# A decoder layer on one core: 28 chunks of u turned during the mixer, none in the gates' stage, and the softmax's maximum taken right behind the last logits

## The chip, the core and the metric

The kernel runs on one NeuronCore of a Trainium2 chip. The core has TensorE (PE in the profile; its weight loads are PEld), VectorE (DVE), ScalarE (ACT), GpSimd (POOL) and SyncE (SP). The metric is the device time of one execution in microseconds (us); lower is better.

## The reference

One layer over 256 tokens of width 1024, in float32:

```python
h = rmsnorm(x, mix_norm_g); proj = h @ w_in          # nine groups of columns
ret = retention(rotary(rq), rotary(rk), rv); y_a = (ret * silu(rg)) @ ret_w_branch
att = moba_attention(norm(mq), norm(mk), mv, rel_bias)   # softmax over 256 keys, 8 heads
y_b = att @ moba_w_branch
x = x + (sigmoid(ga) * y_a + sigmoid(gb) * y_b) @ w_out
h2 = rmsnorm(x, ffn_norm_g)
# product keys: 8 heads, 16 of 128 x 128 experts for each token
a = gelu(einsum('td,thkd->thk', h2, u_tab[experts]))
x = x + einsum('thk,thkd->td', gates * a, v_tab[experts])
```

The tables `peer_u` and `peer_v` hold 16384 rows of 1024 numbers each (64 MB).

## The kernel before, in words

**Stages.** The mixer (0 to about 250 us) computes everything up to the residual. The stage of the queries (to about 297) multiplies by `peer_w_q`. The gates' stage (297 to 638) multiplies the activations with all of `peer_u`, in 128 chunks of 128 experts, for most of the tokens, applies gelu and the gates; the last stage does the same with `peer_v` and ends with the output. For the remaining tokens the rows of their experts are gathered one by one (`fetch`, L1056, issued by POOL; the dot products are on DVE, L1067), six buffers in a ring.

**The mixer's order.** The weights come in pieces of 256 x 512 numbers (0.5 MB). At step `i` of the loop at L851 the program issues, in this order: the loads of pieces up to four ahead (SP, L208, into `raw_ring`, a ring of six buffers), `cut(i + 3)` (the high half of a piece on ACT, L153, the low half on DVE, L154), the products of piece `i` on TensorE (L236 to L238), `early_turns(i)`, and `pump()`, which advances up to three side tasks by one `yield` each. Attention is such a task. Each engine works its instructions off in the order in which they were issued.

**Attention (L356).** For each of two tiles of 128 tokens: the logits of eight heads (L367), the bias added by DVE (L371, a `yield` after each group of heads), in the next step the maximum on DVE (L375) and four exponentials on ACT (L377), then four more, then the transposes of the probabilities on TensorE (L389).

**Chunks of u must be transposed.** Most are turned on TensorE in the gates' stage: `transpose_u(c + 2)` at L1315 gives eight transposes of 128 x 128 (L734) and two copies on ACT (L735), two chunks ahead of the products at L1333. Two other ways spare TensorE this:

- *Turned in the mixer* (`early_turns`, L761): chunk `EARLY[m]` is loaded by four DMAs of POOL (L744) at step `TURNED[m] - 4`, turned by DVE in two halves at steps `TURNED[m]` and the next (L748), and written to the DRAM buffer `turned` by a DMA that ACT issues two steps after `TURNED[m]` (L771). The gates' stage loads it back into `raw_ring` and multiplies straight from there. There are three pairs of buffers in turn (`SLOT`): `eraw` and `eT`; `h2` and `hTf`; and a third that is half of `sa` and half of `ret` at first, and from chunk number `LATE` on the attention's tile `pr`.
- *Turned in the gates' stage* (`TURN`): chunks 124 and 126 are loaded by ACT's queue in quarters, beside the products of chunks 95 to 109 (L1323 to L1328), and turned by DVE (L727).

14 chunks (`HELD`) lie in W from the queries' stage on. The other chunks come through `raw_ring`, in order, by SP (L676, or L699 for those turned early); an early chunk keeps its buffer until its product, two chunks longer than the others.

**The gates' stage beside it.** A list of tasks with due times (`chain_step`) first finds the top experts and then builds the dense gates: one-hot factors on DVE (L1194, L1197) and ACT (L1201), their products on TensorE (L1252, L1253), the evacuation on ACT (L1268) and DVE (L1270), and the product with gelu on POOL (L1285). `gather` issues a little over one row fetch for each chunk.

Of the kernel before, what the change touches and what calls it, by code (L numbers as in the profile page):

```python
# [11 lines left out]
F32 = mybir.dt.float32  # L12
# [7 lines left out]
OP = mybir.AluOpType  # L20
AX = mybir.AxisListType

P = 128
# [3 lines left out]
KC = D // P  # L27
H = 8
# [22 lines left out]
HELD = [0, 1, 2, 8, 14, 21] + list(range(26, 62, 6)) + [61, 66]  # L51
HELD0 = 2
FOLD = 104
TURNED = [8, 10, 12, 14] + list(range(20, 34, 2)) + [37, 40, 42, 45, 47, 50, 52, 55, 57, 60, 62, 65, 67, 70]
NPRE = len(TURNED)
LEAD = 4
LATE = 13
SLOT = [m % 3 for m in range(11)] + [m % 3 for m in range(NPRE - 11)]
EARLY = [c for c in range(3, 121) if c not in HELD]
EARLY = [EARLY[round(m * (len(EARLY) - 1) / (NPRE - 1))] for m in range(NPRE)]  # L60
TURN = (124, 126)
TURN0 = 95
WARM = 8
GROW = 96
VX = 14
# [16 lines left out]
def layer_kernel(ctx, tc, x, mix_norm_g, w_in, ret_w_branch, moba_q_gain, moba_k_gain, moba_w_branch,  # L82
# [33 lines left out]
    def hi_tile(dt=F32R):  # L116
        return rg.tile([P, 1024], dt, name="rhi_", tag="rhi", bufs=4)

    def lo_tile(dt=F32R):
        return rg.tile([P, 1024], dt, name="rlo_", tag="rlo", bufs=4)  # L120
# [235 lines left out]
    def attention():  # L356
        ssum = wk.tile([P, NT, H], F32, name="ssum")
        for t in range(NT):
            w = (t + 1) * P
            pr = wk.tile([P, H, S], F32, name="pr")  # L360
            nh = 512 // w
            for i0 in range(0, 4, nh):
                ps = [side() for _ in range(2)]
                for j in range(nh):
                    for c in range(2):
                        b = slice(c * 64, (c + 1) * 64)
                        T.matmul(ps[c][:, j * w:(j + 1) * w], mqk[0][b, i0 + j, t * P:(t + 1) * P],  # L367
                                 mqk[1][b, i0 + j, :w], start=True, stop=True)
                for c in range(2):
                    n = slice(4 * c + i0, 4 * c + i0 + nh)  # L370
                    V.tensor_tensor(pr[:, n, :w], ps[c].rearrange("p (j k) -> p j k", j=nh),  # L371
                                    bias[:, n, S - w:], op=OP.add)
                    yield
            sm = wk.tile([P, H], F32, name="smx")
            V.tensor_reduce(sm, pr[:, :, :w], axis=AX.X, op=OP.max, negate=True)  # L375
            for h in range(H):
                A.activation(pr[:, h, :w], pr[:, h, :w], AF.Exp, bias=sm[:, h:h + 1], accum_out=ssum[:, t, h:h + 1])  # L377
                if h % 4 == 3:
                    yield
            rs = wk.tile([P, H], F32, name="rs")  # L380
            V.reciprocal(rs, ssum[:, t, :])
            yield
            turned_pr = []
            for kt in range(t + 1):
                prT = t4([P, H, P], "prT")
                for q in range(2):
                    p = side()
                    for j in range(4):
                        T.transpose(p[:, j * P:(j + 1) * P], pr[:, 4 * q + j, kt * P:(kt + 1) * P], ident)  # L389
                    A.activation(prT[:, 4 * q:4 * q + 4, :], p.rearrange("p (j i) -> p j i", j=4), AF.Copy)  # L390
                turned_pr.append(prT)
                yield
            rr, at = [pr[:, 2 * i:2 * i + 2, :].rearrange("p h k -> p (h k)") for i in range(2)]
            A.activation(rr.rearrange("p (i c d) -> p i c d", c=2, d=64),
                         rs.rearrange("p (c i) -> p i c", c=2)[:, :, :, None].to_broadcast([P, 4, 2, 64]), AF.Copy)
            yield
            if t == 0:
                yield
            po, pt = side(), side()
            for i in range(4):  # L400
                T.transpose(pt[:, i * P:(i + 1) * P], rr[:, i * P:(i + 1) * P], ident)
            for kt, prT in enumerate(turned_pr):
                for i in range(4):
                    for c in range(2):
                        h = 2 * i + c
                        T.matmul(po[c * 64:(c + 1) * 64, i * P:(i + 1) * P], mv[:, kt, h * 64:(h + 1) * 64],
                                 prT[:, 4 * c + i, :], start=(kt == 0 and i == 0), stop=(kt == t), skip_group_check=True)
            A.activation(at, pt, AF.Copy)
            yield
            V.tensor_tensor(at, at, po, op=OP.mult)  # L410
            yield
            split_to(ah[0][:, :, t * P:(t + 1) * P], al[0][:, :, t * P:(t + 1) * P],
                     at.rearrange("p (c q) -> p c q", c=4))
            yield
# [268 lines left out]
    def load_any(i):  # L683

        if sk_at <= i < sk_at + 2:
            r = raw_tile().rearrange("p (j i) -> p j i", j=H)
            nc.sync.dma_start(r, peer_sub_keys[0].rearrange("h c n d -> n (h c) d")[:, H * (i - sk_at):H * (i - sk_at + 1), :])
            sk_raw.append(r)
            return
        i -= 2 * (i >= sk_at)  # L690
        if i < len(pieces):
            load(i)
        elif i < len(pieces) + NK:
            c = i - len(pieces)
            if c in HELD or c in TURN:
                return
            if early_chunk(c):
                u_raw[c] = raw_tile()
                nc.sync.dma_start(u_raw[c], turned[EARLY.index(c)])  # L699
            else:  # L700
                u_raw[c] = load_rows(peer_u, c)
        elif i < len(pieces) + 2 * NK:
            c = i - len(pieces) - NK
            n = (c - VX) % (RAWS + 2) - RAWS if c >= VX else -1
            v_raw[c] = load_rows(peer_v, c, spare(n) if n >= 0 else None)
# [13 lines left out]
    def transpose_u(c):  # L719

        if c < NK and early_chunk(c):
            u_T[c] = u_raw.pop(c)
        elif c in TURN:
            r = u_raw.pop(c)
            u_T[c] = hi_tile(F32)
            for k in range(0, KC, 4):
                turn(u_T[c], r, slice(k, k + 4))  # L727
        elif c < NK:
            r = u_raw.pop(c)
            u_T[c] = hi_tile(F32)  # L730
            for q in range(2):
                p = side()
                for k in range(4):
                    T.transpose(p[:, k * P:(k + 1) * P], r.rearrange("p (i k) -> p k i", k=KC)[:, 4 * q + k], ident)  # L734
                A.activation(u_T[c][:, 512 * q:512 * (q + 1)], p, AF.Copy)  # L735

    def early_chunk(c):
        return c in EARLY

# [6 lines left out]
    def turn(dst, src, k):  # L746

        V.transpose(dst.rearrange("p (k b a) -> p b k a", k=KC, b=4)[:, :, k],  # L748
                    src.rearrange("p (b k i) -> p b k i", b=4, k=KC)[:, :, k])
# [561 lines left out]
    for c in range(NK):  # L1311
        load_to(len(pieces) + c + TAHEAD)
        rows_x(c)
        gates_finish()
        transpose_u(c + TAHEAD)  # L1315
        if c and c % 2 == 0:
            product_evac(c - 2, pa)
        if c == SCRATCH:
            while any(g in chain for g in topk_all):
                chain_step(1.0)  # L1320
        if c % 2 == 0:
            pa = acc(0)
        m, g = divmod(c - TURN0, 8)  # L1323
        if 0 <= m < len(TURN) and g % 2 == 0:
            if g == 0:
                assert gs["xdone"]
                u_raw[TURN[m]] = lo_tile(F32)
            load_quarters(nc.scalar, u_raw[TURN[m]], TURN[m], (g // 2,))  # L1328
        uT = u_T.pop(c)
        hT = hTd if c in TURN or early_chunk(c) else hTf  # L1330
        for k in range(KC):
            n = c % 2 * NA
            T.matmul(pa[:, n:n + NA], uT[:, k * P:(k + 1) * P], hT[:, k], start=(c % 2 == 0 and k == 0),  # L1333
                     stop=(k == KC - 1), skip_group_check=True)
        pump()
        if c < NK - 6 or gs["dot"] == NU and (not gs["weighed"] or gs["v"] - gs["sum"] < RING - 1):
            gather(gs["pace"])
        chain_step(BUDGET)

        if c == NK - 4:  # L1340
            while chain:
                chain_step(9.0)
                gates_finish()
            cw = cp.tile([P, 2, D], F32R, name="cw", tag="b8")[:, :, :4 * ND].rearrange("p s (c t) -> p s c t", c=2)
        if c >= NK - 5:
            load_to(len(pieces) + c + 3)
        if c == NK - 3:
            cut_w(0)
            cut_v(0)
        elif c == NK - 2:  # L1350
            cut_v(1)
# [143 lines left out]
```

## Time and profile before

| what | us |
|---|---|
| median of 3 runs | 934.42 (934.07 to 935.47) |
| the profiled execution | 934.2 |
| its span, first to last instruction | 932.4 |
| PE busy | 921.0 |
| DVE busy | 802.0 |
| ACT busy | 511.3 |
| POOL busy | 439.8 |

The page of the profile gives busy times, groups of instructions by line, and the chain of work that ended last. Other views of the same trace show who waited for whom, the instructions in order of time, the busy time of each engine in chosen stretches, and single lines with the landing times of their DMAs. In a row of the order of time, the brackets tell how long the engine had been idle and what ended it. Names of tiles are the program's: `raw_ring` for what SP loaded, `rhi` and `rlo` for the two halves of a piece, `rows` for gathered rows.

### The profile page before, as it was taken

Reading aid. Unit: us, or ns where it says so; the run is one execution under the profiler, and the core shown is the slowest. Engines: PE = TensorE matmul, PEld = TensorE weight load, DVE = VectorE, ACT = ScalarE, POOL = GpSimd, SP = SyncE. Lnnn points to the kernel's source line nnn. Section 1 sums busy time; section 2 is a strip of 40 time slices with the busy share of each in tenths; the row PEclk is TensorE's granted clock in tenths of the full one; section 3 lists DMA queues with packets and bytes.
Section 4 is the critical chain, followed back from the end, with each engine's and each line's share of the span. In section 5 each row is a group of like instructions: output and inputs, shape, how many; then the busy total and the mean of one; then the engine's idle time right before and its main releaser. Section 6 shows DMA issues by size and latency. Waiting matters only on the chain.

```text
span 932.4 us, 18724 instructions
## 1 busy us (share of the span) xinstructions
PE 921.0 (99%) x6960; PEld 874.1 (94%) x6960; DVE 802.0 (86%) x1537; ACT 511.3 (55%) x940; POOL 439.8 (47%) x408
## 2 busy tenths in 40 slices
PE   8999999999999999999999999899999999999998
PEld 6877888888999999999999999899999999999997
DVE  6668666888779999999999989896999989898996
ACT  5455655544644435444677776686454545454543
POOL 3617133321202447435655676674656555555530
PEclk9999999999999999999999999999999999999999
DMA  9999997999799999999999999999999999999991
GB/s 319 222 354 246 342 271 227 351 334 329 240 370 396 408 385 354 386 353 378 408 392 404 370 389 366 390 409 350 371 396 409 409 406 409 385 408 380 386 385 63
DMA packets 108121, 329.88 MB, mean 354 GB/s; under 512 B 12316, under 2 KB 17349, under 8 KB 107902
## 3 DMA queue, kind: packets, MB, share of 16 engines
q1 hardware_dynamic: 65244, 184.12, 54.6%
q0 software_dynamic: 37248, 128.00, 37.5%
q10 hardware_dynamic: 5538, 16.57, 4.6%
q8 instruction: 55, 0.90, 0.4%
q14 instruction: 36, 0.29, 0.1%
HBM read 312.30 MB, written 17.86 MB: 354 GB/s over the span
## 4 chain that ended last, share of the span: by engine, by line
PE 66%; DMA 4%; DVE 1%; POOL 1%; issue 0%; ACT 0%; DVEq 0%; POOLq 0%
PE acc L1333 20%; PE acc L1365 9%; PE side L1365 9%; PE side L734 8%; PE acc L1366 4%; PE side L1366 4%; DMA rows<-in_peer_u_dram,eg 3%; PE side L1363 2%; PE acc L1363 2%; PE acc L246 1%; PE acc L245 1%; PE acc L247 1%; DMA rows__6045<-in_peer_u_dram,eg 1%; PE side L626 1%; DMA gx<-av 1%; PE acc L1252 1%
## 5 line engine op out<-in xcount | busy, mean ns | idle before, releaser
L1056 POOL DMA_INDIRECT rows<-in_peer_u_dram,eg x86 | 104.9, 1220 | 79.4 <-DVE rows L1067 38.5
L1056 POOL DMA_INDIRECT rows<-in_peer_v_dram,eg x54 | 101.3, 1876 | 75.5 <-DVE vacc L1155 59.1
L734 PE MATMUL side<-ident,raw_ring 128*128 128x128 f32 x696 | 93.4, 277 | 0.8 <-DMA raw_ring<-in_peer_u_dram 0.8
L734 PEld LDWEIGHTS side<-ident,raw_ring 128*128 128x128 f32 x696 | 84.3, 192 | 1.1 <-PE acc L1253 0.9
L1299 ACT ACTIVATE cw<-W 128x352 fp32r<-128x352 f32 x58 | 29.0, 499 | 71.1 <-PE acc L1366 71.1
L1067 DVE SCALAR_TENSOR_TENSOR rows<-rows,h 128x1024 f32<-128x1024 f32 x44 | 54.7, 1249 | 6.7 <-DMA rows<-in_peer_u_dram,eg 6.6
L1201 ACT ACTIVATE oh_buf<-oh_more,tS 128x128 bf16<-128x128 f16 x176 | 58.5, 419 | 3.4 <-DVE oh_more L1194 3.3
L1155 DVE SCALAR_TENSOR_TENSOR vacc<-rows,av,vacc 128x1024 f32<-128x1024 f32 x42 | 53.8, 1281 | 0.1
L1333 PE MATMUL acc<-hTd,raw_ring 128*128 128x128 f32 x400 | 48.8, 275 | 0.0
L1333 PEld LDWEIGHTS acc<-hTd,raw_ring 128*128 128x128 f32 x400 | 46.7, 192 | 0.0
L1300 DVE TENSOR_TENSOR cw<-W,cw 128x352 fp32r<-128x352 f32 x58 | 30.3, 522 | 16.5 <-ACT cw L1299 16.0
L1285 POOL TENSOR_TENSOR W<-W,gl 128x256 f32<-128x256 f32 (+21 forms) x32 | 26.6, 830 | 25.1 <-ACT gl L1284 22.9
L744 POOL DMA_DIRECT2D eraw<-in_peer_u_dram x36 | 19.8, 556 | 30.8 <-DVE eT L748 30.8
L1194 DVE TENSOR_TENSOR oh_more<-iota,tI 128x1024 f16<-128x1024 f16 x44 | 33.5, 761 | 0.0
L1197 DVE TENSOR_TENSOR oh_buf<-oh_more,tM 128x1024 f16<-128x1024 f16 x44 | 33.2, 755 | 0.0
L744 POOL DMA_DIRECT2D h<-in_peer_u_dram x36 | 19.7, 554 | 23.1 <-DVE hTf L748 22.8
L1252 PE MATMUL acc<-oh_buf 128*128 128x128 bf16 x176 | 24.4, 219 | 2.7 <-DVE W L1270 2.7
L1268 ACT ACTIVATE W<-acc 128x512 f32<-128x512 f32 (+22 forms) x44 | 17.3, 393 | 17.4 <-PE acc L1253 16.4
L1253 PE MATMUL acc<-oh_buf 128*128 128x128 bf16 x176 | 24.4, 219 | 0.0
L1252 PEld LDWEIGHTS <-oh_buf 128*128 128x128 f16 x176 | 19.8, 113 | 2.9 <-DVE W L1270 2.9
L1287 ACT ACTIVATE W<-acc 128x256 f32<-128x256 f32 (+21 forms) x53 | 18.5, 350 | 4.4 <-PE acc L1333 4.3
L1270 DVE TENSOR_TENSOR W<-acc,W 128x256 f32<-128x256 f32 (+21 forms) x32 | 16.1, 502 | 4.8 <-ACT W L1268 4.8
(2608 smaller groups left out, 3400.7 us busy)
## 6 DMA issues: line engine op xcount, KB each, us to landing
raw_ring<-in_peer_v_dram SPq DMA_DIRECT2D x100, 512.0 KB, 10.1
raw_ring<-in_peer_u_dram SPq DMA_DIRECT2D x87, 512.0 KB, 9.5
raw_ring<-in_w_in_dram SPq DMA_DIRECT2D x52, 512.0 KB, 7.6
W<-in_peer_v_dram SPq DMA_DIRECT2D x28, 512.0 KB, 10.6
raw_ring<-turned SPq DMA_DIRECT2D x25, 512.0 KB, 10.7
raw_ring<-in_peer_w_q_dram SPq DMA_DIRECT2D x16, 512.0 KB, 10.8
W<-in_peer_u_dram SPq DMA_DIRECT2D x14, 512.0 KB, 11.1
eraw<-in_peer_u_dram POOLq DMA_DIRECT2D x36, 128.0 KB, 8.0
```

Source lines behind the costliest of these rows:

```text
L734: T.transpose(p[:, k * P:(k + 1) * P], r.rearrange("p (i k) -> p k i", k=KC)[:, 4 * q + k], ident)
L744: queue.dma_start(dst[32 * g:32 * g + 32].rearrange("a (b d) -> a b d", b=4), src[g])
L1056: G.indirect_dma_start(out=r, out_offset=None, in_=tab, in_offset=bass.IndirectOffsetOnAxis(ap=eg[:, j:j + 1], axis=0))
L1067: V.scalar_tensor_tensor(r, r, 1.0, h, op0=OP.mult, op1=OP.mult, accum_out=av[:, j:j + 1])
L1155: V.scalar_tensor_tensor(a, r, av[:, j:j + 1], a, op0=OP.mult, op1=OP.add)
L1194: V.tensor_tensor(hot, iota4[:, None].to_broadcast(shape), tI[:, t, :, None, k:k + 4].to_broadcast(shape), op=OP.is_equal)
L1201: A.activation(o1[:, j], hot[:, 0, :, j], AF.Copy, scale=tS[:, t, k + j:k + j + 1])
L1252: T.matmul(p[:, j * P:(j + 1) * P], hi, o1, start=True, stop=False)
L1333: T.matmul(pa[:, n:n + NA], uT[:, k * P:(k + 1) * P], hT[:, k], start=(c % 2 == 0 and k == 0), stop=(k == KC - 1), skip_group_check=True)
L1363: T.matmul(o[b][:, :ND], vh[:, n], w, start=False, stop=False, skip_group_check=True)
L1365: T.matmul(o[b][:, :2 * ND], vh[:, n], w, start=(c == 0), stop=False, skip_group_check=True)
L1366: T.matmul(o[b][:, :ND], vl[:, n], w[:, :ND], start=False, stop=(c == NK - 1), skip_group_check=True)
```

## The change

The list of steps `TURNED` gets 16, 18 and 34, so 28 chunks are turned during the mixer instead of 25. `LATE` and `SLOT` are shifted by three, so the last 14 chunks keep their steps and buffers. `EARLY` is drawn from the chunks 3 to 125 instead of 3 to 120: before it was 3, 7, 13, 18, 24, 29, 34, 40, 45, 51, 55, 62, 67, 71, 76, 80, 85, 89, 94, 98, 102, 107, 111, 116, 120; after it is 3, 7, 12, 17, 22, 28, 33, 37, 42, 47, 52, 57, 62, 67, 72, 76, 80, 84, 88, 92, 96, 100, 104, 109, 113, 117, 121, 125. `TURN` is gone: chunks 124 and 126 come through the ring and are turned on TensorE. In attention, the maximum is issued right behind the last addition of the bias, one step earlier; the exponentials stay where they were.

```diff
--- before.py
+++ after.py
@@ -51,15 +51,13 @@
 HELD = [0, 1, 2, 8, 14, 21] + list(range(26, 62, 6)) + [61, 66]
 HELD0 = 2
 FOLD = 104
-TURNED = [8, 10, 12, 14] + list(range(20, 34, 2)) + [37, 40, 42, 45, 47, 50, 52, 55, 57, 60, 62, 65, 67, 70]
+TURNED = list(range(8, 36, 2)) + [37, 40, 42, 45, 47, 50, 52, 55, 57, 60, 62, 65, 67, 70]
 NPRE = len(TURNED)
 LEAD = 4
-LATE = 13
-SLOT = [m % 3 for m in range(11)] + [m % 3 for m in range(NPRE - 11)]
-EARLY = [c for c in range(3, 121) if c not in HELD]
+LATE = 16
+SLOT = [m % 3 for m in range(14)] + [m % 3 for m in range(NPRE - 14)]
+EARLY = [c for c in range(3, 126) if c not in HELD]
 EARLY = [EARLY[round(m * (len(EARLY) - 1) / (NPRE - 1))] for m in range(NPRE)]
-TURN = (124, 126)
-TURN0 = 95
 WARM = 8
 GROW = 96
 VX = 14
@@ -370,9 +368,10 @@
                     n = slice(4 * c + i0, 4 * c + i0 + nh)
                     V.tensor_tensor(pr[:, n, :w], ps[c].rearrange("p (j k) -> p j k", j=nh),
                                     bias[:, n, S - w:], op=OP.add)
+                    if n.stop == H:
+                        sm = wk.tile([P, H], F32, name="smx")
+                        V.tensor_reduce(sm, pr[:, :, :w], axis=AX.X, op=OP.max, negate=True)
                     yield
-            sm = wk.tile([P, H], F32, name="smx")
-            V.tensor_reduce(sm, pr[:, :, :w], axis=AX.X, op=OP.max, negate=True)
             for h in range(H):
                 A.activation(pr[:, h, :w], pr[:, h, :w], AF.Exp, bias=sm[:, h:h + 1], accum_out=ssum[:, t, h:h + 1])
                 if h % 4 == 3:
@@ -692,7 +691,7 @@
             load(i)
         elif i < len(pieces) + NK:
             c = i - len(pieces)
-            if c in HELD or c in TURN:
+            if c in HELD:
                 return
             if early_chunk(c):
                 u_raw[c] = raw_tile()
@@ -720,11 +719,6 @@

         if c < NK and early_chunk(c):
             u_T[c] = u_raw.pop(c)
-        elif c in TURN:
-            r = u_raw.pop(c)
-            u_T[c] = hi_tile(F32)
-            for k in range(0, KC, 4):
-                turn(u_T[c], r, slice(k, k + 4))
         elif c < NK:
             r = u_raw.pop(c)
             u_T[c] = hi_tile(F32)
@@ -1320,14 +1314,8 @@
                 chain_step(1.0)
         if c % 2 == 0:
             pa = acc(0)
-        m, g = divmod(c - TURN0, 8)
-        if 0 <= m < len(TURN) and g % 2 == 0:
-            if g == 0:
-                assert gs["xdone"]
-                u_raw[TURN[m]] = lo_tile(F32)
-            load_quarters(nc.scalar, u_raw[TURN[m]], TURN[m], (g // 2,))
         uT = u_T.pop(c)
-        hT = hTd if c in TURN or early_chunk(c) else hTf
+        hT = hTd if early_chunk(c) else hTf
         for k in range(KC):
             n = c % 2 * NA
             T.matmul(pa[:, n:n + NA], uT[:, k * P:(k + 1) * P], hT[:, k], start=(c % 2 == 0 and k == 0),
```

## The prediction

> **What bounds the kernel now.** I read the page first, then the busy time by stages, then who made TensorE wait.
>
> ```profile
> span 932.4 us, 18724 instructions
> PE 921.0 (99%) x6960; PEld 874.1 (94%) x6960; DVE 802.0 (86%) x1537; ACT 511.3 (55%) x940; POOL 439.8 (47%) x408
> ```
>
> ```profile
> 50.00:62.00 12.00, 11.77 (x54) 9.53 (x53) 7.36 (x10) 5.74 (x16) 0.00 (x0) 1.00 1.04 369
> ```
>
> ```profile
> 297.00:520.00 223.00, 223.00 (x2060) 223.00 (x2059) 215.08 (x681) 122.79 (x286) 117.32 (x111) 1.00 0.99 385
> ```
>
> ```profile
> 555.00:591.00 36.00, 32.50 (x317) 32.06 (x316) 30.49 (x51) 23.35 (x71) 25.06 (x21) 1.00 1.03 370
> 591.00:638.00 47.00, 47.00 (x463) 47.00 (x462) 38.71 (x61) 34.37 (x88) 31.28 (x29) 1.00 1.03 396
> ```
>
> ```profile
> PE acc L1252 <- DVE W L1270: 2.7, 1, 2.7
> PE side L734 <- DMA raw_ring<-in_peer_u_dram: 0.8, 1, 0.8
> ```
>
> The columns of the second to fourth fence are the stretch, its length, busy time of PE, PEld, DVE, ACT and POOL, the granted clock, the DMA share and GB/s. The clock is 1.00 throughout. TensorE is idle for 11 us in all (932.4 less 921.0), and in most of the gates' stage (297 to 638) it never stops. So a PE instruction that goes away is worth its time, unless a wait of TensorE takes its place. Three waits matter here: the two of the last fence, in the gates' stage at 580 and 589, in a stretch where PE is busy 32.50 of 36 us; and one in the mixer's softmax, shown in part 2. In all these stretches the 16 DMA engines are full (share 0.99 to 1.04), and DVE is busy 215 of 223 us: these two are what can take a gain back.
>
> **Part 1: one chunk fewer for TensorE to turn.** A chunk that was not turned ahead costs eight transposes.
>
> ```profile
> L734 PE MATMUL side<-ident,raw_ring x696: 272/274/348, 304.1 to 637.5; 128*128 128x128 f32 x174
> ```
>
> ```profile
> L734 PE MATMUL side<-ident,W x112: 272/273/282, 296.1 to 461.2; 128*128 128x128 f32 x112
> ```
>
> ```profile
> 517.09 0.95 PE side L734 x8
> ```
>
> 696 + 112 = 808 transposes are 101 chunks: 128 less the 25 turned in the mixer and the two of TURN. After the change it is 128 - 28 = 100. The row of the chain gives 0.95 us for the eight, since their 274 ns overlap. So **-0.95 us**. [...]
>
> Where it falls matters. By the lists in the code, up to chunk 110 (the one turned at 590) EARLY holds 22 chunks before and 24 after; from 111 on, 5 need no turning before (three of EARLY and the two of TURN) and 4 after. TensorE is therefore two chunks, 1.9 us, earlier when it comes to the waits at 580 and 589, and gives one chunk back behind them. ACT loses two copies of a chunk; it is not the bound. DVE loses the four turns of TURN behind chunks 124 and 126, in the stretch from 591 on, where PE waits for nothing (47.00 of 47) and DVE is busy 38.71: worth nothing.
>
> **Part 2: the maximum.** The first softmax is the one that TensorE feels.
>
> ```profile
> 61.17 0.60 PE L389 MATMUL side<-ident,pr 128*128 128x128 f32 x4
> 62.14 1.49 PE L389 MATMUL side<-ident,pr 128*128 128x128 f32 x4 [0.38 <-ACT pr L377]
> 63.38 0.48 PE L236 MATMUL acc<-rhi__594,hh 128*128 128x512 f32 x1
> ```
>
> ```profile
> 50.45 0.70 DVE L748 STREAM_TRANSPOSE hTf<-h 128x512 f32<-128x512 f32 x1
> ...
> 53.58 0.65 DVE L371 TENSOR_TENSOR pr<-side,bias 128x512 f32<-128x512 f32 x1
> 56.12 1.22 DVE L154 TENSOR_TENSOR rlo__571<-raw_ring,rhi__570 128x1024 fp32r<-128x1024 f32 x1 [1.89 <-ACT rhi__570 L153]
> 57.26 0.70 DVE L748 STREAM_TRANSPOSE ret<-sa 128x512 f32<-128x512 f32 x1
> 57.89 1.18 DVE L375 TENSOR_REDUCE smx<-pr 128x8 f32<-128x1024 f32 x1
> ```
>
> ```profile
> 55.02 1.06 ACT L153 ACTIVATE rhi__570<-raw_ring 128x1024 fp32r<-128x1024 f32 x1 [3.25 <-DMA raw_ring<-in_w_in_dram]
> 59.10 0.40 ACT L377 ACTIVATE pr<-pr,smx 128x128 f32<-128x128 f32 x1 [3.01 <-DVE smx L375]
> ...
> 60.66 1.05 ACT L153 ACTIVATE rhi__594<-raw_ring 128x1024 fp32r<-128x1024 f32 x1
> ```
>
> The eight transposes of the probabilities take 2.21 us (61.17 to 63.38) in place of 0.95: 1.26 us lost, because the second four wait head by head for exponentials, and ACT had stood 3.01 us for the maximum. Right behind the add the maximum runs from 54.2 to 55.4, inside DVE's idle 1.89 us before 56.12, so it costs DVE nothing and delays nobody queued behind it. The first four exponentials (1.56 us, 59.10 to 60.66) then run at 56.1 to 57.7, and ACT stands ready for the weights rhi__594 at 57.7 instead of 60.66. In the second tile the same move takes ACT's other wait; PE shows no wait for it, so nothing. Alone this part is worth **-1.3 us**.
>
> **Part 3: two more chunks turned in that very place.** Steps 16 and 18 are new, so their loads are issued by POOL at steps 12 and 14, when the buffers come free: behind DVE's turn out of `h`, done at 51.2 (50.45 + 0.70), and behind that out of `sa`, done at 58.0 (57.26 + 0.70). (The third, step 34, loads near 100 us, where no PE wait shows.)
>
> ```profile
> L208 SPq DMA_DIRECT2D raw_ring<-in_w_in_dram x1: 367/367/367, 39.8 to 39.8; - x1
> ...
> DMA to landing us min/median/max: 19.0/19.0/19.0
> ```
>
> POOL was idle from 50 to 62 (0.00 busy), so its 8 issues are free. The DMA engines are not: the weights of rhi__594, issued at 39.8, land at 58.8 after 19 us. Two chunks are 1 MB, at 369 GB/s 2.8 us of all engines. If the first (1.4 us) gets ahead of those weights, they land at 60.2; ACT cuts them before exponentials 4 to 7, which end near 62.8 instead of 63.1. Then nearly all of part 2 is gone again, though ACT is no later than before. If the loads run in gaps, all 1.3 stay. [...]
>
> DVE gets 4 turns more between 66 and 78, 4 x 0.70 = 2.8 us, ahead of the low halves of the weights:
>
> ```profile
> 68.60 1.17 DVE L154 TENSOR_TENSOR rlo__652<-raw_ring,rhi__651 128x1024 fp32r<-128x1024 f32 x1
> ```
>
> ```profile
> 69.82 0.50 PE L237 MATMUL acc<-rlo__652,hh 128*128 128x512 f32 x1
> ```
>
> PE takes rlo__652 0.05 us after DVE makes it: no slack there, and the new turns come right behind it. The maximum that left 57.89 makes DVE up to 1.2 us earlier just before. And ACT issues the write of each turned chunk two steps on, after waiting for the turn; behind it on ACT stand the next weights' high halves. I take a mean for parts 2 and 3 together: **-0.4 us**, between -1.3 (no crowding) and +1.5 (both loads, 2.8 us, ahead of the weights, less the 1.3).
>
> **Part 4: 1 MB leaves the stretch in which the gates' stage waits.**
>
> ```profile
> L744 ACTq DMA_DIRECT2D rlo__6078<-in_peer_u_dram x4: 318/342/354, 549.8 to 566.0; - x4
> L744 ACTq DMA_DIRECT2D rlo__6389<-in_peer_u_dram x4: 317/334/347, 572.7 to 591.3; - x4
> ```
>
> ```profile
> 523.45 0.52 PE side L734 x4
> ...
> 526.32 0.63 POOL W L1285
> ...
> 570.78 14.80 DMA rows<-in_peer_u_dram,eg
> ```
>
> ```profile
> 585.61 1.79 DVE L1067 SCALAR_TENSOR_TENSOR rows<-rows,h 128x1024 f32<-128x1024 f32 x1 [1.47 <-DMA rows<-in_peer_u_dram,eg]
> ```
>
> ```profile
> rows<-in_peer_u_dram,eg POOLq DMA_INDIRECT x86, 8.5
> ```
>
> TURN's eight loads, 128 KB each, are issued between 549.8 and 591.3, in a stretch with the DMA engines at 1.03. The chain to the 2.7 us wait at 589 goes through gathered rows that took 14.80 us from issue to landing (median 8.5), and DVE stood 1.47 us for them; the 0.8 us at 580 is a chunk of u that landed late. After the change this 1 MB, 2.8 us of DMA time at 370 GB/s, is loaded by SP among the last chunks instead, where PE has no wait (591 to 638: 47.00 of 47). A shorter queue can give back at most both waits, 3.5 us; the 1.47 and the 0.8, 2.3 us, are what the late landings cost directly. Against it, TensorE comes 1.9 us earlier. The chain starts from PE work at 523, through POOL's product L1285, so it should come earlier too, but not wholly, since POOL and DVE have their own pace. I take **-1.2 us**; ends -3.5 (both waits gone) and +1.9 (DVE's chain stays where it was and TensorE waits its whole lead).
>
> **Sum.** The profiled execution took 934.2 us, its span 932.4 and 1.8 around it; the median of the runs is 934.42, 0.2 more. -0.95 - 0.4 - 1.2 = -2.55: 931.6 for an execution like the profiled one, **931.8** for the median.
>
> **The rivals.**
> *A, the lead is eaten (same).* DVE and the gathers set the time at 589, so TensorE waits longer by what it came earlier. For it: DVE is busy 96% from 297 to 520, the row's wait is for DVE. Against it: the chain begins with PE at 523, and 1 MB less is queued. With part 4 at 0 to +0.9, the sum is -0.95 - 0.4 + 0.45 = -0.9: 933.5.
> *B, the mixer's weights come late (slower).* The two loads at 51 and 58 get ahead of the weights of steps 16 to 19, and TensorE waits for rhi__594 and its successors. For it: the share of 1.04, landings after 19 us, no slack at 69.8. It decides once rhi__594 lands later than about 60.5. Against it: late as these weights land, they cost PE nothing so far; ACT had waited for the maximum instead. With +1.5 there, +0.5 for the turns that delay rlo, and part 4 at +0.9: -0.95 + 2.0 + 0.9 = +1.95: 936.4.
> *C, everything lands.* No crowding (-1.3) and both waits gone (-3.5): -0.95 - 4.8 = -5.75: 928.7. For it: both causes are named in the rows. Against it: gathers that wait for POOL remain.
>
> **Numbers.** The forecast 0.42, A 0.34, B 0.16, C 0.08. A measurement of this kernel can tell some 0.2%, 1.9 us: faster means under 932.55, slower over 936.29. The forecast's own range, 930 to 933.3, lies mostly on the faster side: 0.38 of its 0.42, the rest is same. Of A 0.04 are faster, 0.29 same, 0.01 slower; of B 0.04 are same and 0.12 slower; C is faster. So faster 0.50, same 0.37, slower 0.13. The range 929.2 to 936.3 leaves out most of C and the far half of B.
>
> **What would show it.** Right: L734 has 800 transposes; the eight of L389 near 61 us end within 1.5 us; no ACT wait for smx; the rows issued near 570 land in under 11 us, and PE's waits on L1252 and L734 together are under 2 us. Wrong: PE waits on L236 or L237 between 58 and 75 for weights (B); PE's wait on L1252 of 4 us or more (A); a new wait of PE between 610 and 640, where SP now loads the two chunks.

## The result and the profile after

| | before | after |
|---|---|---|
| median, us | 935.37 (934.07 to 936.86, 8 runs) | 930.95 (929.76 to 931.66, 8 runs) |
| profiled execution, us | 934.2 | 930.9 |
| its span, us | 932.4 | 929.1 |

The ratio of the medians is 0.995, with a 95% interval of 0.9939 to 0.9961: faster by 3.6 to 5.7 us, where 2.6 was forecast. The two profiled executions are 3.3 us apart. The changed kernel was timed twice more among the experiments, against the kernel before on the same chip: 0.9972 (0.9952 to 0.9993; 932.29 against 935.01) and 0.9958 (0.9944 to 0.9972; 931.93 against 935.17), so 2.6 and 3.9 us by the ratio. By the three ratios the gain is 2.6 to 4.7 us.

The page of the profile after, its span and busy times:

```profile
span 929.1 us, 18724 instructions
PE 919.9 (99%) x6952; PEld 873.2 (94%) x6952; DVE 801.4 (86%) x1539; ACT 510.7 (55%) x938; POOL 447.8 (48%) x420
```

TensorE has eight instructions fewer and 1.1 us less work (919.9 against 921.0); it is idle for 9.2 us in place of 11.4. So two thirds of the gain are waits that went. The busy times by stretch, after, in the columns of the prediction's fences, show where:

```profile
50.00:62.00 12.00, 11.86 (x55) 9.62 (x53) 7.70 (x9) 5.70 (x14) 4.36 (x8) 1.00 1.04 349
```

```profile
555.00:591.00 36.00, 36.00 (x357) 36.00 (x356) 32.85 (x56) 25.77 (x78) 27.17 (x22) 1.00 1.02 406
591.00:638.00 47.00, 46.30 (x450) 46.13 (x449) 34.82 (x52) 33.84 (x83) 31.26 (x27) 1.00 1.01 387
```

From 555 to 591 TensorE now works all 36.00 us (32.50 before), and the same DMA engines move 406 GB/s in place of 370. From 591 to 638, where it waited for nothing, it now lacks 0.70 us. Its waits in the gates' stage, after (time waited, times, longest), and that one in the order of time:

```profile
PE side L728 <- DMA raw_ring<-in_peer_u_dram: 0.7, 1, 0.7
```

```profile
633.24 1.13 PE L728 MATMUL side<-ident,raw_ring 128*128 128x128 f32 x8 [0.70 <-DMA raw_ring<-in_peer_u_dram]
```

Both waits of before are gone, 3.5 us, and a new one stands at 633, at one of the last chunks that SP loads. (Lines have moved up by a few: L734 is L728 now, L389 is L388, L377 is L376, L1252 is L1246.) The transposes are as counted:

```profile
L728 PE MATMUL side<-ident,raw_ring x688: 272/274/348, 304.7 to 634.1; 128*128 128x128 f32 x172
```

```profile
L728 PE MATMUL side<-ident,W x112: 272/273/282, 296.7 to 460.8; 128*128 128x128 f32 x112
```

688 + 112 = 800, a hundred chunks.

The mixer gained nothing; it lost. TensorE at the first softmax, after:

```profile
61.27 0.60 PE L388 MATMUL side<-ident,pr 128*128 128x128 f32 x4
62.65 1.49 PE L388 MATMUL side<-ident,pr 128*128 128x128 f32 x4 [0.79 <-ACT pr L376]
63.90 0.48 PE L234 MATMUL acc<-rhi__598,hh 128*128 128x512 f32 x1
```

The eight transposes take 2.63 us (61.27 to 63.90); they took 2.21. (Two later profiles of the same kernel, those of experiments 5 and 11, have 2.80 and 2.77.) DVE and ACT after show why:

```profile
54.74 1.22 DVE L373 TENSOR_REDUCE smx<-pr 128x8 f32<-128x1024 f32 x1
56.40 1.23 DVE L152 TENSOR_TENSOR rlo__577<-raw_ring,rhi__576 128x1024 fp32r<-128x1024 f32 x1 [0.44 <-ACT rhi__576 L151]
```

```profile
55.30 1.06 ACT L151 ACTIVATE rhi__576<-raw_ring 128x1024 fp32r<-128x1024 f32 x1 [3.05 <-DMA raw_ring<-in_w_in_dram]
56.27 0.38 ACT L376 ACTIVATE pr<-pr,smx 128x128 f32<-128x128 f32 x1
61.16 1.06 ACT L151 ACTIVATE rhi__598<-raw_ring 128x1024 fp32r<-128x1024 f32 x1 [3.25 <-DMA raw_ring<-in_w_in_dram]
62.12 0.38 ACT L376 ACTIVATE pr<-pr,smx 128x128 f32<-128x128 f32 x1
```

The maximum did move into DVE's idle time (54.74, only 0.44 us of it left), and the exponentials start at 56.27 without a wait for it, where they started at 59.10. But then ACT stands 3.25 us for the weights rhi__598 (the piece that was called rhi__594 before), which land at 61.1 and not at 58.8, though SP issued them at 39.8 in both kernels. The second four exponentials are queued behind that cut and start at 62.12. A wait for a maximum was exchanged for a wait for weights. At the mixer's end TensorE is 0.56 us late. Before:

```profile
248.56 1.13 PE L589 MATMUL side<-ident,hn 128*128 128x128 f32 x8 [0.41 <-DVE hn L579]
```

After:

```profile
249.12 0.57 PE L588 MATMUL side<-ident,hn 128*128 128x128 f32 x3 [0.41 <-DVE hn L578]
```

So by the two profiles: -0.95 for the chunk, +0.56 in the mixer, and -3.5 + 0.7 = -2.8 in the gates' stage make -3.2; the spans differ by 3.3.

The theory to test had three parts: the maximum alone is worth about 1 us, but not beside the new loads; the gates' waits went because 1 MB left that stretch, and would go from the kernel before as well; the mixer's loss comes from the loads of the chunks at steps 16 and 18. The rivals: the waits went because TensorE came at other times, or the mixer's weights came late for another reason.

### The profile page after: what moved, and what is told of

It is laid out like the page before. It is cut to its first block, busy times and chain, and to the rows that moved or that the text cites. A ratio compares the mean times of both kernels' runs of the same rounds, so it can differ in the third digit from the quotient of the medians.

```text
span 929.1 us, 18724 instructions
## 1 busy us (share of the span) xinstructions
PE 919.9 (99%) x6952; PEld 873.2 (94%) x6952; DVE 801.4 (86%) x1539; ACT 510.7 (55%) x938; POOL 447.8 (48%) x420
## 4 chain that ended last, share of the span: by engine, by line
PE 72%; DMA 1%; DVE 0%; ACT 0%; issue 0%; DVEq 0%
PE acc L1321 24%; PE side L728 10%; PE acc L1353 10%; PE side L1353 9%; PE acc L1354 4%; PE side L1354 4%; PE side L1351 2%; PE acc L1351 2%; PE acc L244 1%; PE acc L243 1%; PE acc L245 1%; PE acc L1247 1%; PE acc L1246 1%; DMA raw_ring<-in_peer_u_dram 1%; PE side L625 1%; PE side L894 0%
## 5 line engine op out<-in xcount | busy, mean ns | idle before, releaser
L1050 POOL DMA_INDIRECT rows<-in_peer_u_dram,eg x86 | 107.3, 1247 | 75.0 <-DVE rows L1061 29.8
L1050 POOL DMA_INDIRECT rows<-in_peer_v_dram,eg x54 | 95.6, 1770 | 77.8 <-DVE vacc L1149 59.9
L728 PE MATMUL side<-ident,raw_ring 128*128 128x128 f32 x688 | 92.3, 277 | 0.7 <-DMA raw_ring<-in_peer_u_dram 0.7
L728 PEld LDWEIGHTS side<-ident,raw_ring 128*128 128x128 f32 x688 | 83.3, 192 | 0.9 <-issue 0.9
L1321 PE MATMUL acc<-hTd,raw_ring 128*128 128x128 f32 x448 | 54.6, 275 | 0.0
L1321 PEld LDWEIGHTS acc<-hTd,raw_ring 128*128 128x128 f32 x448 | 52.3, 192 | 0.0
L738 POOL DMA_DIRECT2D eraw<-in_peer_u_dram x40 | 21.9, 554 | 39.2 <-DVE eT L742 39.2
L738 POOL DMA_DIRECT2D h<-in_peer_u_dram x40 | 21.8, 552 | 34.2 <-DVE hTf L742 26.2
L1246 PE MATMUL acc<-oh_buf 128*128 128x128 bf16 x176 | 24.4, 219 | 0.0
L1281 ACT ACTIVATE W<-acc 128x256 f32<-128x256 f32 (+21 forms) x53 | 18.5, 349 | 5.5 <-PE acc L1321 5.4
L1246 PEld LDWEIGHTS <-oh_buf 128*128 128x128 f16 x176 | 19.8, 114 | 0.0
L1247 PEld LDWEIGHTS <-oh_buf 128*128 128x128 f16 x176 | 19.7, 114 | 0.0
```

What stands on the lines that cost most here:

```text
L738: queue.dma_start(dst[32 * g:32 * g + 32].rearrange("a (b d) -> a b d", b=4), src[g])
L1050: G.indirect_dma_start(out=r, out_offset=None, in_=tab, in_offset=bass.IndirectOffsetOnAxis(ap=eg[:, j:j + 1], axis=0))
L1246: T.matmul(p[:, j * P:(j + 1) * P], hi, o1, start=True, stop=False)
L1247: T.matmul(p[:, j * P:(j + 1) * P], lo, o1, start=False, stop=True)
```

## The experiments

**1. The maximum alone.** The kernel before with the moved maximum and nothing else.

```diff
+                    if n.stop == H:
+                        sm = wk.tile([P, H], F32, name="smx")
+                        V.tensor_reduce(sm, pr[:, :, :w], axis=AX.X, op=OP.max, negate=True)
                     yield
-            sm = wk.tile([P, H], F32, name="smx")
-            V.tensor_reduce(sm, pr[:, :, :w], axis=AX.X, op=OP.max, negate=True)
```

> The kernel before with the maximum moved and nothing else. Theory: without the two extra loads the weights of step 17 land at 58.8 as before, the first four exponentials end near 57.7 and the last four near 61.4, and TensorE's eight transposes at 61 us end by 62.2 instead of 63.4: 1.3 us less than before, with the waits at 580 and 589 left as they are. Rival: TensorE waits for the weights there and not for the maximum, so that the move is worth nothing alone: 0.

Measured: 933.70 against 935.59, ratio 0.9984 (0.9964 to 1.0004). TensorE in the order of time, this kernel:

```profile
61.62 1.16 PE L390 MATMUL side<-ident,pr 128*128 128x128 f32 x8
62.54 0.48 PE L236 MATMUL acc<-rhi__594,hh 128*128 128x512 f32 x1
```

Eight transposes in one go, 0.92 us from the first to the next instruction, so the price of 1.3 us was right where nothing crowds the weights. At the mixer's end TensorE is 0.8 us earlier than before (247.79 against 248.56), and not 1.3, since a new wait of 0.40 us, which ends at 46.80, takes part of it: there TensorE stands for a copy that is behind the weights of step 13 on ACT.

```profile
247.79 1.14 PE L590 MATMUL side<-ident,hn 128*128 128x128 f32 x8 [0.41 <-DVE hn L580]
```

The time alone does not settle it (the interval includes a ratio of 1); the rows do. The gates' wait is still there, and now longer:

```profile
PE acc L1253 <- DVE W L1271: 3.1, 1, 3.1
```

**2. The change without the maximum.** The reverse of that edit, on the kernel after.

> The kernel after with the maximum back in its old place, one step later. Theory: in the kernel after, exponentials 4 to 7 stand behind the weights that land at 61.1, and a maximum at 58 to 59 lets the first four end at 60.7, before that; so the same time as after, 4.4 us less than before, within 0.4. Rival: the move is worth its 1.3 us in the kernel after too, and this one comes out 3.1 us less than before.

Measured: 932.43 against 935.59, ratio 0.9952 (0.9929 to 0.9974), beside 0.9950, 0.9972 and 0.9958 of the kernel after. In the changed kernel the moved maximum gives nothing that these runs can tell. The gain is in the chunks.

**3. The kernel before without TURN.** Its two chunks come through the ring and TensorE turns them: 103 chunks, two more than before; the mixer stays.

```diff
-TURN = (124, 126)
+TURN = ()
```

> The kernel before without TURN: chunks 124 and 126 come through the ring and are turned on TensorE, 25 chunks stay turned early, in the same steps; the mixer is as before. Theory (TURN's 1 MB of loads between 550 and 591 made the gathered rows late): two chunks more to turn cost 1.9 us, the waits at 580 and 589 give back 2.3 to 3.5, so 0.4 to 1.6 us less than before. Rival (the waits come from where the early chunks lie and from DVE's pace): 1.9 us more than before.

Measured: 933.01 against 935.59, ratio 0.9974 (0.9957 to 0.9991), with 16 transposes and 1.6 us *more* work on TensorE (busy 922.5 us against 921.0). This kernel's busy times in the stretch of the waits:

```profile
555.00:591.00 36.00, 36.00 (x357) 36.00 (x356) 33.91 (x56) 25.86 (x77) 26.57 (x23) 1.00 1.00 389
```

36.00 of 36, and its list of waits of TensorE from 297 to 640 is empty. The list EARLY is that of before, and the two chunks that TensorE now turns come behind the waits, so no later or earlier arrival by the spread of the chunks can explain it. Turning two chunks on DVE cost more in waits than it spared TensorE.

**4. The loads put back.** The kernel after, with the eight loads of 128 KB that TURN issued, at the same chunks and on the same queue, into tiles that nobody reads.

```diff
+        m, g = divmod(c - 95, 8)
+        if 0 <= m < 2 and g % 2 == 0:
...
+            load_quarters(nc.scalar, u_raw[-1 - m], (124, 126)[m], (g // 2,))
```

> The kernel after, and the eight loads of chunks 124 and 126 by ACT's queue put back beside chunks 95 to 109, into buffers that nobody reads; everything else as after. Theory (these loads make the waits): the rows issued there land late again, and 2 to 3.5 us of the 4.4 are lost. Rival (the new places of the early chunks removed the waits): the same as after, within 0.5 us.

Measured: 934.89 against 935.59, ratio 0.9988 (0.9969 to 1.0006). Most of the gain is gone, with nothing computed more: it is 2.5 us slower than experiment 2 on the same chip, whose gates' stage is that of the kernel after. (The two intervals overlap a little; its span is 931.3, against 929.1 to 929.6 in the three profiles of the kernel after.) This kernel's wait of TensorE, its busy times, and DVE's longest wait for rows:

```profile
PE acc L1246 <- DVE W L1264: 1.8, 1, 1.8
```

```profile
555.00:591.00 36.00, 34.07 (x332) 33.76 (x332) 31.90 (x55) 24.15 (x73) 23.90 (x20) 1.00 1.03 377
```

```profile
581.79 1.63 DVE L1061 SCALAR_TENSOR_TENSOR rows<-rows,h 128x1024 f32<-128x1024 f32 x1 [1.63 <-DMA rows<-in_peer_u_dram,eg]
```

The wait for the gates is back, 1.8 us long, and so is DVE's stop for gathered rows (1.63 us; after, the longest there is 1.00). So the loads make the wait for the gates, and DVE's stop points to the gathers as the way. It is not the whole of the 3.5 us: 1.8 us come back, and the 0.8 us at 580 do not. This trace has no landing times of the gathers; the issues from 560 to 580 of the kernels before and after have them, as the last number, the median time to landing. Before:

```profile
rows<-in_peer_u_dram,eg POOLq DMA_INDIRECT x6, 14.5
```

After:

```profile
rows<-in_peer_u_dram,eg POOLq DMA_INDIRECT x6, 9.9
```

**5. The kernel after once more**, as a control beside the next two.

> The kernel after unchanged, as the measure for the two others of this call on the same chip: 4 to 5 us less than before; a wait of 0.5 to 1.8 us at the transposes near 62 us.

Measured: 932.29 against 935.01, 0.9972 (0.9952 to 0.9993).

**6. 28 chunks, but none at steps 16 and 18.** They are fitted in later in the mixer.

```diff
-TURNED = list(range(8, 36, 2)) + [37, 40, 42, 45, 47, 50, 52, 55, 57, 60, 62, 65, 67, 70]
+TURNED = [8, 10, 12, 14] + list(range(20, 34, 2)) + [35, 37, 41] + list(range(43, 71, 2))
...
-LATE = 16
-SLOT = [m % 3 for m in range(14)] + [m % 3 for m in range(NPRE - 14)]
+LATE = 13
+SLOT = [m % 3 for m in range(11)] + [m % 3 for m in range(NPRE - 11)]
```

> The kernel after with 28 chunks turned early as well, but none in steps 16 and 18: the steps are 8 to 14 and 20 to 32 as before, then 35, 37, 41 and every second one from 43 to 69. The gates' stage is that of the kernel after. Theory (the two loads at 51 and 58 take the maximum's gain away): the weights of step 17 land near 59, the eight transposes near 61 us end by 62.5, and the time is 1 to 1.8 us less than after. Rival (the denser steps from 41 on crowd the weights there in the same way, or the maximum is worth nothing): the same as after or up to 1 us more.

Measured: 934.35 against 935.01, ratio 0.9995 (0.9975 to 1.0015), 2.1 us slower than the control, with intervals that overlap; the two profiles differ by 0.3 (spans 929.7 and 929.4). The wait at 62 is gone: the eight transposes take 0.92 us, against 2.80 in the control, with the same moved maximum. But two new waits stand at 206:

```profile
206.10 0.63 PE L540 MATMUL side<-ident,sa 128*128 128x128 f32 x4 [0.85 <-DVE sa L534]
207.42 0.63 PE L540 MATMUL side<-ident,sa 128*128 128x128 f32 x4 [0.70 <-DVE sa L534]
```

So the maximum is worth its price where the two loads are absent, and the rival fits the time: that part of the mixer has no room either. DVE is late with an addition that TensorE needs, 1.55 us in all.

**7. 29 chunks the same way**: the last part of the list is `list(range(42, 72, 2))`.

> As the last one, with 29 chunks turned early (step 35, 37, 41 and every second one from 42 to 70): TensorE turns 99 chunks. Theory: one chunk less is 0.95 us less than the last one, so 2 to 2.7 less than after. Rival (TensorE's lead is eaten by the waits for DVE and gathers in the gates' stage): the same as the last one.

Measured: 935.47 against 935.01, ratio 1.0005 (0.9979 to 1.0031), 3.2 us slower than the control. The longest of TensorE's waits from 40 to 640:

```profile
PE side L540 <- DVE sa L534: 2.8, 2, 2.1
PE side L365 <- ACT mqk L278: 2.6, 1, 2.6
PE acc L1246 <- ACT oh_buf L1195: 1.0, 1, 1.0
```

One chunk fewer for TensorE to turn gave no gain: the waits at L540 alone (2.8 us) are more than its 0.95. (The 2.6 us at L365 stand ahead of every step that this edit changes; the last section comes back to them.)

**8. 28 chunks spread otherwise**, to see whether the turns in steps 59 to 63 make the wait at L540: there the list is 57, 60, 62, 65, 67, 70 again, and the chunks stand closer ahead of it.

```diff
+TURNED = [8, 10, 12, 14] + list(range(20, 34, 2)) + [35, 37, 40, 41, 43, 45, 47, 49, 51, 53, 55, 57, 60, 62, 65, 67, 70]
...
+LATE = 14
+SLOT = [m % 3 for m in range(11)] + [0, 1] + [(0, 2, 1)[m % 3] for m in range(NPRE - 13)]
```

> 28 chunks turned early, none in steps 16 and 18, and other than in the run with the later steps the places from 57 on are those of the kernel after (57, 60, 62, 65, 67, 70); between, 35, 37, 40, 41 and every second step from 43 to 55. Theory (the wait near 206 us there came from turns in the steps 59 to 63, beside branch A's additions; the wait near 62 from the loads of steps 16 and 18): both waits are gone, and the time is 1.3 to 1.9 us less than after. Rival (any denser steps give their time back): the same as after.

Measured: 934.09 against 935.17, ratio 0.9979 (0.9959 to 0.9998), 2.2 us slower than the control (experiment 11, 931.93), with intervals that overlap. The wait near 62 is gone here too. This kernel at the other place:

```profile
209.00 0.63 PE L540 MATMUL side<-ident,sa 128*128 128x128 f32 x4 [1.43 <-DVE sa L534]
```

The guess fell: the wait is as long. Which of the later turns makes DVE late there stays open.

**9. Without the load of step 16's chunk, and 10. without that of step 18's**; one execution each, to see which of the two delays the weights. The second has `m != 5` in this line:

```diff
-            if step == -LEAD:
+            if step == -LEAD and m != 4:
```

> The kernel after without the four loads of the chunk that is turned in step 16 (POOL, near 52 us); the turn and the write stay and work on stale data, so this chunk's products are left wrong. Theory (this load goes ahead of the weights of step 17): these weights land near 59 instead of 61.1, and TensorE waits at most 0.6 us beyond the plain eight transposes near 62 us. Rival (the load of step 18's chunk, issued at 58.5, is what delays them): they land at 61 as in the kernel after, wait 1.8 us.

> The kernel after without the four loads of the chunk that is turned in step 18 (POOL, near 58.5 us); its products are left wrong. Theory: the weights of step 17 land at 60.5 to 61.1 as in the kernel after, and the wait near 62 us stays at 1.3 to 1.8 us; only the weights after them land 1 us or more earlier. Rival: they land near 59.5 and the wait is under 0.6 us.

Measured: 932.26 and 931.77. ACT at the weights of step 17, first without step 16's load, then without step 18's:

```profile
60.84 1.04 ACT L151 ACTIVATE rhi__594<-raw_ring 128x1024 fp32r<-128x1024 f32 x1
```

```profile
62.38 1.06 ACT L151 ACTIVATE rhi__598<-raw_ring 128x1024 fp32r<-128x1024 f32 x1 [3.00 <-PE acc L235]
```

The landing times themselves do not compare with those of the kernel after: in the first execution TensorE had waited 2.41 us at 48.9, behind the weights of step 13, and all that follows is shifted. What compares is the time from SP's issue of these weights to their landing. SP's issue in the first:

```profile
L206 SPq DMA_DIRECT2D raw_ring<-in_w_in_dram x1: 367/367/367, 42.3 to 42.3; - x1
```

The landing in the second, issued at 41.6:

```profile
DMA to landing us min/median/max: 20.7/20.7/20.7
```

In the first, ACT finds the weights there at 60.84 (no bracket), so they took at most 18.5 us. In the second they took 20.7, and landed at 62.3, where ACT takes them; the kernel after has 21.3 (39.8 to 61.1), and 20.8 in experiment 5. The kernel before has 19.0, and experiments 6 and 8, with neither load, 19.8 and 18.2. So the load of step 16, issued at 52, is what delays them, and not the one at 58.

**11. The kernel after a third time**, beside experiments 8 to 10.

> The kernel after unchanged, as the measure for the others of this call: 3 to 4.5 us less than before.

Measured: 931.93 against 935.17, 0.9958 (0.9944 to 0.9972).

**12. Two loads moved out of the way.** If the weights of step 17 land late because too much is queued ahead of them, another load can go. SP loads two tables at steps 8 and 12 that are used much later.

```diff
-        if i == 8:
+        if i == 20:
             nc.sync.dma_start(decay, c_decay)
-        if i == 12:
+        if i == 40:
             nc.sync.dma_start(grow2, row(ffn_norm_g))
```

> The kernel after with two loads of SP moved away from the crowded stretch: the decay table (512 KB) from step 8 to step 20, the second norm's gain (512 KB) from step 12 to step 40; nothing else. Theory (the DMA engines are the bound from 20 to 62 us, and every 512 KB there delays the weights behind it): the weights of step 13 land before 44 and those of step 17 before 59, the waits of TensorE near 47 and 62 go, and the time is 1.3 to 2.5 us less than that of the kernel after, 4.5 to 6.5 less than before. Rival (the stretch is bound by the small rows of the bias table, whatever else is queued): the weights land as in the kernel after, and so does the time.

Measured: **929.14** against 934.84, ratio 0.9937 (0.9918 to 0.9956), span 926.4. This is less than the kernel before. Against the kernel after it was not timed side by side, only through the kernel before (0.9937 against 0.9950, 0.9972 and 0.9958, with intervals that overlap); its span is 2.7 us under the shortest of that kernel's three (929.1, 929.4 and 929.6). ACT and TensorE in its mixer:

```profile
43.52 1.06 ACT L151 ACTIVATE rhi__478<-raw_ring 128x1024 fp32r<-128x1024 f32 x1 [5.02 <-DMA raw_ring<-in_w_in_dram]
58.04 1.06 ACT L151 ACTIVATE rhi__596<-raw_ring 128x1024 fp32r<-128x1024 f32 x1 [1.44 <-DMA raw_ring<-in_w_in_dram]
```

```profile
61.25 1.03 PE L388 MATMUL side<-ident,pr 128*128 128x128 f32 x8
62.04 0.48 PE L234 MATMUL acc<-rhi__596,hh 128*128 128x512 f32 x1
```

The weights land 3.1 us earlier (58.0), the eight transposes take 0.79 us from the first to the next instruction, and the mixer ends 2.2 us earlier than after:

```profile
246.90 1.13 PE L588 MATMUL side<-ident,hn 128*128 128x128 f32 x8 [0.41 <-DVE hn L578]
```

All 28 turns and the moved maximum are in this kernel, so neither of them was wrong for its place; what was wrong was what stood ahead of the weights. That is more than bytes on the way. SP's issue of these weights and their time to landing, here:

```profile
L206 SPq DMA_DIRECT2D raw_ring<-in_w_in_dram x1: 368/368/368, 37.7 to 37.7; - x1
...
DMA to landing us min/median/max: 20.2/20.2/20.2
```

They took 20.2 us in place of 21.3, but were issued at 37.7 in place of 39.8: two thirds of the 3.1 us are the earlier issue. In the kernel after, the gain (L850) is issued by SP right ahead of them, at 38.5, and both issues stand for a load of the bias table to land, the gain's 1.8 us and the weights' another 0.9:

```profile
SPq L850 <- DMA bias<-skew: 1.8, 1, 1.8
```

So the rival was not all wrong: the bias table has a part in it, though not "whatever else is queued". Which of the two tables matters, and whether by its bytes or by its place in SP's order, was not separated.

## Why the prediction was right, and which sizes were off

The side, and the mechanism of each part, held; two terms were off, in opposite directions. By the profiles the mixer came out 0.96 us worse than forecast and the gates' stage 1.6 us better; that the sum is off by no more than 0.6 (-3.2 against -2.55) is in part luck.

- *Part 1, -0.95.* Right: 800 transposes, and TensorE 1.1 us less busy.
- *Parts 2 and 3, -0.4 taken.* Measured: +0.56 at the mixer's end. This term was off in size and in sign, by the step "I take a mean for parts 2 and 3 together". The sentence ahead of it had the mechanism ("If the first gets ahead of those weights"), priced by bytes: 1.4 us for the first load, a landing at 60.2, exponentials done near 62.8. The weights landed at 61.1, 2.3 us late in place of 1.4, and the last exponentials start at 62.12 and end at 63.66. Experiment 1 shows that the maximum alone is worth the predicted amount in the softmax, experiment 2 that the times show nothing of it beside the loads, experiment 6 that it is back without them, experiments 9 and 10, one execution each, that it is step 16's load. A mean between two ends was taken where the evidence (a DMA share of 1.04, a landing after 19 us) spoke for one of them. The turns on DVE were no trouble: no new wait stands at rlo near 70.
- *Part 4, -1.2 taken.* Measured: -2.8 (3.5 us of waits gone, 0.7 new), near the lower end of -3.5. The direct cost of the late landings (2.3 us) was taken as the gain and then cut for the earlier arrival of TensorE. But without the 1 MB the gathers of that stretch land sooner (a median of 9.9 us in place of 14.5; the prediction asked for under 11), and DVE, held for at most 1.00 us at one, has the gates ready for a TensorE that comes earlier: no wait for them is left at all. Experiment 3 shows that the two waits go without any change of the early chunks, experiment 4 that 1.8 us of them come back with the loads alone. For the rest, the 0.8 us at 580 among it, it stays open how much is the loads and how much the new places of the early chunks.
- *The rivals.* A needed TensorE's earlier arrival to be eaten at 589: with the loads put back (experiment 4) part of it is, without them it isn't. B came in mildly: weights late, but 2.3 us, and TensorE felt it through the exponentials and not at L234. C was right in the gates' stage and wrong in the mixer. The wait "between 610 and 640, where SP now loads the two chunks" came, at 633, and took 0.70.

The profiles add up to 3.2 of their 3.3 us. The first pair of medians differs by 4.4. Part of the rest may be the clock: of 86 executions of the kernel before, timed beside experiments 1 to 11, 27 had a mean granted clock that rounds to 1.000, with medians of 933.2 to 934.2 us in the three timings, and 59 a lower one, with medians of 936.3 to 936.7. Of the kernel after, one of 8 executions had a lower one in the first timing, but 8 of 12 in each of the later two. A link between a wait and the clock is seen in single profiles (below); that it makes the difference of the medians wasn't tested and stays open.

## What to carry to other kernels

A wait of the bounding engine can be the end of a chain that begins at full DMA engines, as the waits at 589 and at 62 were (a DMA share of 1.03 from 555 to 591, of 1.04 from 50 to 62): bytes that leave the stretch ahead of the wait can be worth more than the work that they fed (experiment 3: 3.5 us of waits gone for 1.6 us of work), and bytes that come into a stretch where weights land just in time can cost more than their share of bandwidth (here 2.3 us in place of an estimated 1.4). A late landing has two parts, when the load was issued and how long it took; read both. Before an engine's idle time is filled with a step whose data must be loaded, look at what lands late there already, and first move away loads that are needed much later. And when a wait is removed, read what stands next in that engine's queue: here the exponentials passed from waiting for a maximum to waiting behind a cut of weights.

## What the runs showed of the hardware

After a wait of TensorE of 2.4 to 3.1 us, four profiles show the granted clock at half for 3.4 us (experiments 1, 2, 7 and 9). Experiment 1, behind its wait of 3.1 us (the clock is the third number from the end):

```profile
585.00:588.70 3.70, 0.60 (x6) 0.41 (x6) 3.57 (x6) 0.53 (x2) 3.15 (x3) 1.00 1.03 394
588.70:592.10 3.40, 3.40 (x21) 3.40 (x22) 3.40 (x6) 2.67 (x7) 1.15 (x1) 0.50 1.03 371
592.10:596.00 3.90, 3.90 (x40) 3.90 (x40) 3.35 (x6) 1.55 (x6) 2.30 (x3) 1.00 1.04 399
```

21 matmuls in 3.40 us, and 40 in the 3.90 behind them: 3.4 us at half speed are, as an estimate, 1.7 us lost on top of the wait. The same stood behind the waits of 2.59 us in experiment 2 (a clock of 0.50 over 3.4 us), 2.6 in experiment 7 (0.51) and 2.41 in experiment 9 (0.50); but not behind the 2.7 us at 589 of the kernel before, nor behind the 2.7 us of experiment 8: the mean granted clock of these two profiles is 1.000, that of the four 0.998. Experiment 2, behind its wait, and the kernel before, in its wait and behind it:

```profile
51.50:54.90 3.40, 3.40 (x9) 2.63 (x9) 2.42 (x3) 2.93 (x5) 0.73 (x2) 0.50 1.05 296
```

```profile
586.90:589.70 2.80, 0.11 (x2) 0.04 (x2) 2.80 (x6) 0.50 (x2) 2.30 (x2) 1.00 1.03 395
589.70:593.10 3.40, 3.40 (x35) 3.40 (x36) 3.40 (x6) 3.40 (x11) 1.89 (x2) 1.00 1.03 365
```

So a wait of 2.4 to 2.7 us cost its own length in two profiles and, by the estimate of 1.7 us, 4.1 to 4.3 in three others. Its length alone doesn't tell them apart (2.41 us with the half clock, 2.7 without it); what does was not shown, since no run moved a wait.

ACT took the weights of step 13 at 43.5 us in experiment 12, at 44.2 in the kernel before, at 44.7 in the kernel after, at 47.5 in experiment 7 and at 48.5 in experiment 2, each time straight from a wait for their landing: the landing moves from one profile to the next, with kernels that are alike up to there but for the tables of experiment 12. At its late end TensorE waits 2.4 to 2.7 us near 50 (experiments 2, 7, 8 and 9), since a copy that it needs stands behind those weights on ACT. By these waits, and the 1.7 us estimated above where the half clock follows, single profiles of these kernels differ by 2 to 4 us in a place that no edit touched, and an edit is better judged at its own place than by the span.
